# Attention products cut from 256 to 128 moving columns in a hybrid transformer layer

## The chip, the cores and the metric

The kernel runs on one core of a Trainium2 chip. The metric is the device time of one execution in microseconds (us). A lower time is better. All times of the profile come from one profiled execution, counted from its first instruction.

## The reference

One layer of a hybrid encoder on 512 tokens of width 1024, all in float32. What matters here is the token mixing: one input projection, three groups of attention heads of width 64, and one output projection.

```python
def reference(x, p, ln_mix, w_in, ...):
    hn = rms_norm(h, ln_mix[i])
    z = hn @ w_in[i]                      # columns of all head groups
    (q1, q2, k1, k2, va, qf, kf, vf, fg, qc, kc, vc) = jnp.split(z, IN_SPLITS, axis=-1)
    ...
    o_a = diff_attention(q1, q2, k1, k2, va, lam, subln_g, lam_init)   # 4 heads, two softmax maps each
    o_b = forgetting_attention(qf, kf, vf, log_f)                      # 6 heads, causal
    o_c = chunk_attention(qc, kc, vc, rel_bias[i])                     # 6 heads, chunk-causal
    h = h + jnp.concatenate([o_a, o_b, o_c], axis=-1) @ w_out[i]
    h = h + conv_gated_mlp(rms_norm(h, ln_ffn[i]), ...)                # width 2816, causal conv of width 3
    gate = jax.nn.sigmoid(rms_norm(h, ln_ple[i]) @ w_ple_gate[i])
    return h + (p[i] @ w_ple_proj[i]) * gate
```

Each attention is softmax(q k + bias) v with a mask that lets a token see its own block of 128 tokens (cut by the mask) and the blocks before it, and no later block.

## The kernel before, in words

**Stages.** The first stage multiplies the normalised input by the combined projection, runs the attention, and adds the output projection. The second is the gated MLP, and the last the gate with the per-layer embedding. The attention is spread over the projections of the first stage: while the projection of one pair of heads runs on TensorE, the attention of earlier pairs is mixed into the same stream. The pairs are A0, A1, B0, B1, B2, C0, C1 and C2, two heads each, so there are 16 heads.

**Precision.** Almost every product is made with operands of type float32r (`F32R`), each number split into a high part (names with `h`, `hi` or `th`) and a rest (`l`, `lo` or `tl`), and summed over two or three matmuls. In the profile `z<-whi,Th` is a matmul into the PSUM tile `z` with `whi` as the moving operand and `Th` as the stationary one. The profile shows the operands of F32R and of plain float32 alike as `f32`. Plain float32 is used by the transposes (moving operand `ident`) and by one small product, `o<-otmp,oall` in `subln` (line 966), which sums squares for the heads of group A and moves 512 columns.

**Scores** (`softmax_map`, lines 855 to 877). For a block `qb` of 128 queries, the keys up to `L = (qb + 1) * P` matter, with `P = 128`. Two matmuls write the scores to a bank `s`: one with the keys `k`, one with their rests `kl`. They move `N = max(L, 256)` key columns, so the first query block moves 256 columns, though only the first 128 are read afterwards. There are 8 such maps for each query block in group A (two maps for each of 4 heads), 6 in B and 6 in C: 20 in all, and so 40 matmuls for each of the four query blocks.

**Values** (`prob_cols` and `values`, lines 905 to 955). The probabilities are transposed to columns by key block. Key blocks 0 and 1 get tiles `pth` and `ptl` of their own (512 and 384 columns). Key blocks 2 and 3 share the tiles `ptc[0]` (high parts) and `ptc[1]` (rests): columns 0 to 127 hold zeros, written once at the start by two ScalarE activations (lines 834 and 835), columns 128 to 255 the one block of queries that sees key block 3, columns 256 to 511 the two that see key block 2. `values` sums the products of the four key blocks in one bank `o`, two matmuls for each key block. For key block 3 it moves columns 0 to 255 of `ptc`, zeros first, to columns 256 to 511 of `o` (`off = min(kb, 2) * P`). So each of the 16 heads has four matmuls from `ptc`, all 256 columns wide.

**What sets the order.** The class `Plan` records the operations of the first stage with their dependencies and then chooses an order for each engine, in `solve`. `price` (lines 194 to 227) gives each operation a duration; that of an F32R matmul is `n * 0.0004556 + 0.001` us for `n` moving columns, whatever `n` is. `due` gives every TensorE operation a due time from the sum of the durations ahead of it, plus a number for its group from the table `SHIFT`; the other engines' due times follow back from there. `emit` then issues all instructions in the order chosen, and each engine works through its own in that order. The later stages have a second plan, which takes over the clocks and memory of the first.

Of the kernel before, what the change touches and what calls it, by code (L numbers as in the profile page):

```python
# [11 lines left out]
AF = mybir.ActivationFunctionType  # L12
# [3 lines left out]
P = 128  # L16
# [309 lines left out]
def kernel(ctx: ExitStack, tc: tile.TileContext, x, xt0, xt, pt_in, small, g_ffn_in, bias_c,  # L326
# [8 lines left out]
    def f32(ap):  # L335
        return ap.bitcast(F32)
# [31 lines left out]
    pe, act, dve, pool, sp = (Engine(*e) for e in (("pe", nc.tensor), ("act", nc.scalar), ("dve", nc.vector), ("pool", nc.gpsimd), ("sp", nc.sync)))  # L368
# [45 lines left out]
    def bank(tag, name):  # L414
        return banks.tile([P, 512], F32, tag, {"z": 2, "s": 2, "t": 3, "o": 1}[tag])
# [14 lines left out]
    ident = cp.tile([P, P], F32, tag="ident", name="ident")  # L430
# [162 lines left out]
    for b in range(2):  # L593
        for i in range(2):
            c = HALF[1 - i]
# [11 lines left out]
    def done(*key):  # L607
        DONE.add(key)

    def need(*keys):  # L610
        for key in keys:
            assert key in DONE, key
# [218 lines left out]


    ptc = [ap.tile([P, S], F32R, tag=f"ptc{b}", name=f"ptc{b}") for b in range(2)]
    for b in range(2):
        act.activation(ptc[b][:, 0:P], ident, AF.Copy, scale=0.0)

    def head_bias(kind, hd):

# [15 lines left out]

    def softmax_map(m, hh, qb, bias, rowb, name):
        L = (qb + 1) * P
        N = max(L, 256)
        q, k, kl = m[0][hh], m[1][hh], m[2]
        c = slice(qb * P, L)
        sp = bank("s", f"{name}_s")  # L860
        pe.matmul(sp[:, :N], q[:, c], k[:, :N], start=True, stop=False)
        pe.matmul(sp[:, :N], q[:, c], kl[hh][:, :N], start=False, stop=True)
        e = ap.tile([P, L], F32, tag=f"e{qb}", bufs=2, name=f"{name}_e")
        st = ap.tile([P, 4], F32, tag="st", bufs=12, name=f"{name}_st")
        init = 3.0e38
        for n, (c0, tab) in enumerate(bias):
            c = slice(c0, c0 + tab.shape[1])
            acc = st[:, 3 * n : 3 * n + 1]
            dve.tensor_tensor_reduce(out=e[:, c], in0=sp[:, c], in1=tab, scale=-1.0, scalar=init,
                                           op0=ALU.add, op1=ALU.min, accum_out=acc)  # L870
            init = acc
        if rowb is not None:
            dve.scalar_tensor_tensor(st[:, 0:1], init, rowb, rowb, ALU.subtract, ALU.add)
            init = st[:, 0:1]
        act.activation(e, e, AF.Exp, scale=-1.0, bias=init, accum_out=st[:, 1:2])
        dve.reciprocal(st[:, 2:3], st[:, 1:2])
        return e, st
# [3 lines left out]
    def scores(pr, hh, qbs):  # L881
        kind, i = pr[0], int(pr[1])
        hd = 2 * i + hh
        if kind == "B":
            need(("fc",))
        if (pr, hh) not in BIAS:
            BIAS[pr, hh] = head_bias(kind, hd)
            PROB[pr, hh] = []
        for qb in qbs:
            bq = BIAS[pr, hh](qb)  # L890
            rowb = fq[:, qb, hd : hd + 1] if kind == "B" else None
            e, st = softmax_map(QK[pr, 0], hh, qb, bq, rowb, f"{pr}_{hh}_{qb}")
            if kind == "A":
                yield
                e2, st2 = softmax_map(QK[pr, 1], hh, qb, bq, rowb, f"{pr}_{hh}_{qb}b")
                pool.tensor_scalar(e2, e2, st2[:, 2:3], X["nlam"], ALU.mult, ALU.mult)
                dve.scalar_tensor_tensor(e, e, st[:, 2:3], e2, ALU.mult, ALU.add)
            else:
                pool.tensor_scalar(e, e, st[:, 2:3], 1.0, ALU.mult, ALU.mult)
            PROB[pr, hh].append(e)  # L900
            if hh == 1 and qb == NT - 1:
                KL_FREE.extend(QK[pr, part][2] for part in range(2) if (pr, part) in QK)
            yield

    def prob_cols(pr, hh):
        probs = PROB[pr, hh]
        tiles = []
        for kb in range(2):
            n = (NT - kb) * P
            pt = bank("t", f"{pr}_{hh}_pt{kb}")  # L910
            for qb in range(kb, NT):
                pe.transpose(pt[:, (qb - kb) * P : (qb - kb + 1) * P], probs[qb][:, kb * P : (kb + 1) * P], ident)
            th = ap.tile([P, S], F32R, tag="pth", bufs=3, name=f"{pr}_{hh}_pth{kb}")
            tl = ap.tile([P, S], F32R, tag="ptl", bufs=3, name=f"{pr}_{hh}_ptl{kb}")
            act.copy(th[:, :n], pt[:, :n])
            dve.tensor_tensor(out=tl[:, :n], in0=pt[:, :n], in1=f32(th[:, :n]), op=ALU.subtract)
            tiles.append((th[:, :n], tl[:, :n]))
            yield
        assert not PTC_OF
        PTC_OF.append((pr, hh))  # L920
        pt = bank("t", f"{pr}_{hh}_ptc")
        pe.transpose(pt[:, P : 2 * P], probs[3][:, 3 * P : 4 * P], ident)
        pe.transpose(pt[:, 2 * P : 3 * P], probs[2][:, 2 * P : 3 * P], ident)
        pe.transpose(pt[:, 3 * P : 4 * P], probs[3][:, 2 * P : 3 * P], ident)
        th, tl = ptc
        act.copy(th[:, P:], pt[:, P:])
        dve.tensor_tensor(out=tl[:, P:], in0=pt[:, P:], in1=f32(th[:, P:]), op=ALU.subtract)
        tiles.append((th[:, 2 * P :], tl[:, 2 * P :]))
        tiles.append((th[:, : 2 * P], tl[:, : 2 * P]))
        PT[pr, hh] = tiles  # L930
        yield

    def values(pr, hh):
        need(*(("in", pr, 0, t) for t in range(NT)))
        if pairs.index(pr) >= 6:
            need(("split", pairs.index(pr) - 6))
        if hh == 0:
            O[pr] = oall[:, pairs.index(pr) % 6, :]
        base = hh * HD
        po = bank("o", f"{pr}_{hh}_po")  # L940
        for kb in range(NT):
            off = min(kb, 2) * P
            v = V[pr][:, kb, hh * P : (hh + 1) * P]
            for j in range(2):
                pe.matmul(po[:, off:], v, PT[pr, hh][kb][j], start=kb == 0 and j == 0, stop=kb == 3 and j == 1)
            if kb % 2 == 1 and kb < 3:
                yield
        PTC_OF.remove((pr, hh))
        other = HD - base
        tmp = ap.tile([P, S], F32, tag="otmp", bufs=1, name=f"{pr}_{hh}_ot")  # L950
        act.copy(tmp[base : base + HD, :], po[other : other + HD, :])
        dve.tensor_tensor(out=O[pr][base : base + HD, :], in0=po[base : base + HD, :],
                                in1=tmp[base : base + HD, :], op=ALU.add)
        done("o" if kind_done(pr) else "o_raw", pr, hh)
        yield

    def kind_done(pr):
        return pr[0] != "A"
# [107 lines left out]
    for pr in ("A0", "A1"):  # L1066
        add(pr + "s01", scores, pr, 0, (0, 1))
        add(pr + "s02", scores, pr, 0, (2, 3))
        add(pr + "p0", prob_cols, pr, 0)
        add(pr + "v0", values, pr, 0)  # L1070
        add(pr + "s11", scores, pr, 1, (0, 1))
        add(pr + "s12", scores, pr, 1, (2, 3))
        add(pr + "p1", prob_cols, pr, 1)
        add(pr + "v1", values, pr, 1)
        add(pr + "n", subln, pr)
    for pr in ("B0", "B1", "B2", "C0", "C1", "C2"):
        add(pr + "v1", values, pr, 1)
    for pr in ("B0", "B1", "B2", "C0", "C1", "C2"):
        add(pr + "a", qk_cols, pr, 0)
        add(pr + "s0", scores, pr, 0, range(NT))  # L1080
        add(pr + "s1", scores, pr, 1, range(NT))
        add(pr + "p0", prob_cols, pr, 0)
        add(pr + "v0", values, pr, 0)
        add(pr + "p1", prob_cols, pr, 1)
# [17 lines left out]
    for j, (pr, part, *_) in enumerate(PARTS[1:], 1):  # L1102
        n = w_in[j].shape[3]
        for t in range(NT):
            run(f"in{j}_{t}", in_unit(pr, part, n, t, ws), steps.get(slot, []))
            slot += 1
            if slot >= 37:
                c = slice((slot - 37) * P, (slot - 36) * P)
# [3 lines left out]
        if j + 1 < len(PARTS):  # L1112
            q = PARTS[j + 1]
# [923 lines left out]
    while ready:  # L2037
        q = ready.pop()
# [26 lines left out]
    while order:  # L2065
# [3 lines left out]
        if now:  # L2069
            q = now[0]  # L2070
        else:
            tr = [(trial(q)[0], q) for q in can]
            first_at = max(min(x for x, _ in tr), clock["dve"])
            q = min((q for x, q in tr if x <= first_at + 0.1), key=lambda q: q.dl)

            late = min((q for x, q in tr if x <= first_at + SLACK), key=lambda q: q.dl)
            q = late if late.dl < q.dl - URGENT else q
# [70 lines left out]
```

## Time and profile before

| | us |
|---|---|
| median of 3 runs | 699.09 (698.72 to 699.47) |
| span of the profiled execution, first to last instruction | 697.6 |
| what lies outside the span (median less span) | about 1.5 |
| TensorE busy (PE) | 687.9 of 697.6 |
| VectorE busy (DVE) | 572.9 |
| ScalarE busy (ACT) | 423.5 |
| GpSimd busy (POOL) | 310.5 |

The profile gives the profiled execution's span and no separate time around it, so the median of the runs stands beside it. PE is TensorE's matmul stream and PEld its weight loads, which lie beside matmuls. The length of a single matmul record covers its way through the array, and neighbours overlap; what a matmul costs the stream is read from the distance between the starts of two records. Every instruction that goes through the recording layer has the line 360, so operations are told apart by their tiles.

### The profile page before, as it was taken

Reading aid. Unit: us, or ns where it says so; the run is one execution under the profiler, and the core shown is the slowest. Engines: PE = TensorE matmul, PEld = TensorE weight load, DVE = VectorE, ACT = ScalarE, POOL = GpSimd, SP = SyncE. Lnnn points to the kernel's source line nnn. Section 1 sums busy time; section 2 is a strip of 40 time slices with the busy share of each in tenths; the row PEclk is TensorE's granted clock in tenths of the full one; section 3 lists DMA queues with packets and bytes.
Section 4 is the critical chain, followed back from the end, with each engine's and each line's share of the span. In section 5 each row is a group of like instructions: output and inputs, shape, how many; then the busy total and the mean of one; then the engine's idle time right before and its main releaser. Section 6 shows DMA issues by size and latency. Waiting matters only on the chain.

```text
span 697.6 us, 12855 instructions
## 1 busy us (share of the span) xinstructions
PE 687.9 (99%) x4600; PEld 643.3 (92%) x4600; DVE 572.9 (82%) x1159; ACT 423.5 (61%) x812; POOL 310.5 (45%) x418
## 2 busy tenths in 40 slices
PE   7999999999999999999999999999999999999997
PEld 7999999999999888899988999898998898999997
DVE  6688899888887873888996988789898899777867
ACT  6657676666675672766755544556536676446853
POOL 3677676756764661222231333421622502344561
PEclk9999999999999999999999999999999999999999
DMA  9543354413222152585865338764368654132433
GB/s 310 204 128 92 87 149 129 110 64 92 88 62 72 61 114 98 192 240 127 218 162 145 110 93 224 162 187 129 93 176 224 169 159 128 48 105 67 150 117 122
DMA packets 42989, 94.31 MB, mean 135 GB/s; under 512 B 4871, under 2 KB 9607, under 8 KB 42925
## 3 DMA queue, kind: packets, MB, share of 16 engines
q1 hardware_dynamic: 35868, 79.02, 35.8%
q0 software_dynamic: 6768, 14.16, 11.6%
q8 instruction: 36, 0.59, 0.4%
q10 hardware_dynamic: 288, 0.30, 0.1%
q14 instruction: 29, 0.23, 0.1%
HBM read 85.20 MB, written 4.21 MB: 128 GB/s over the span
## 4 chain that ended last, share of the span: by engine, by line
PE 96%; DVE 1%; POOL 1%; DMA 0%; ACT 0%; issue 0%; POOLq 0%
PE z L360 45%; PE s L360 23%; PE t L360 20%; PE o L360 8%; DMA zn<-in_w_in_dram 0%; DVE xh_again L360 0%; POOL rs L360 0%; POOL e L360 0%; DVE xl_again L360 0%; DVE kl L360 0%; DVE rs L360 0%; ACT xh_again L360 0%; POOL wlo L360 0%; DVE oall L360 0%; ACT sq L360 0%
## 5 line engine op out<-in xcount | busy, mean ns | idle before, releaser
L360 ACT CAST whi<-wraw 128x768 fp32r<-128x768 f32 (+2 forms) x146 | 108.4, 761 | 49.2 <-DMA wraw<-in_w_up_dram 10.6
L360 DVE TENSOR_TENSOR wlo<-wraw,whi 128x768 fp32r<-128x768 f32 (+2 forms) x128 | 112.8, 893 | 18.1 <-ACT whi L360 16.2
L360 PE MATMUL z<-whi,Th 128*128 128x384 f32 (+2 forms) x360 | 120.3, 346 | 4.8 <-ACT whi L360 4.6
L360 PE MATMUL z<-wlo,Th 128*128 128x384 f32 (+2 forms) x360 | 119.6, 342 | 0.0
L360 PE MATMUL z<-whi,Tl 128*128 128x384 f32 (+2 forms) x360 | 119.3, 341 | 0.0
L360 PEld LDWEIGHTS z<-whi,Th 128*128 128x128 f32 x360 | 67.8, 190 | 8.4 <-ACT whi L360 4.9
L360 PEld LDWEIGHTS z<-whi,Tl 128*128 128x128 f32 x360 | 67.8, 189 | 2.9
L360 PEld LDWEIGHTS z<-wlo,Th 128*128 128x128 f32 x360 | 68.1, 190 | 2.3
L360 POOL TENSOR_TENSOR wraw<-wraw,wraw 128x768 f32<-128x768 f32 (+2 forms) x21 | 28.1, 1343 | 82.7 <-DVE pin L360 41.0
L360 ACT ACTIVATE e<-e,st 128x128 f32<-128x128 f32 (+3 forms) x80 | 44.6, 559 | 16.6 <-DVE st L360 16.3
L360 PE MATMUL z<-Th,whi 128*128 128x256 f32 (+1 forms) x152 | 51.8, 341 | 0.0
L360 PE MATMUL z<-Tl,whi 128*128 128x256 f32 (+1 forms) x152 | 51.6, 340 | 0.0
L360 PE MATMUL z<-Th,wlo 128*128 128x256 f32 (+1 forms) x152 | 51.5, 340 | 0.0
L360 PE MATMUL s<-Tl,whi 128*128 128x256 f32 (+1 forms) x152 | 51.5, 340 | 0.0
L360 PE MATMUL s<-Th,wlo 128*128 128x256 f32 (+1 forms) x152 | 51.3, 340 | 0.0
L360 PE MATMUL s<-Th,whi 128*128 128x256 f32 (+1 forms) x152 | 51.1, 341 | 0.0
L360 POOL TENSOR_TENSOR rs<-rs,nhalf 128x4 f32<-128x4 f32 x40 | 43.2, 1090 | 4.9 <-DVE rs L360 1.4
L360 DVE CUSTOM_DVE_ANT_0 e<-s,bias 128x128 f32<-128x128 f32 (+3 forms) x74 | 33.9, 471 | 5.4 <-PE s L360 2.8
L360 POOL TENSOR_SCALAR e<-e,st 128x256 f32<-128x256 f32 (+3 forms) x48 | 29.1, 641 | 10.3 <-DVE st L360 8.3
L360 POOL DMA_DIRECT2D wraw<-in_w_up_dram x21 | 18.9, 902 | 31.4 <-DMA wraw<-in_w_up_dram 21.4
L360 PE MATMUL t<-whi,al 128*128 128x256 f32 x116 | 32.2, 282 | 0.0
L360 PE MATMUL t<-wlo,ah 128*128 128x256 f32 x116 | 32.1, 281 | 0.0
(342 smaller groups left out, 2286.6 us busy)
## 6 DMA issues: line engine op xcount, KB each, us to landing
wraw<-in_w_up_dram SPq DMA_DIRECT2D x41, 384.0 KB, 4.5
wraw<-in_w_in_dram SPq DMA_DIRECT2D x28, 384.0 KB, 3.6
wraw<-in_w_down_dram SPq DMA_DIRECT2D x17, 384.0 KB, 3.2
wlo_again<-in_w_up_dram SPq DMA_DIRECT2D x12, 384.0 KB, 4.3
whi_again<-in_w_up_dram SPq DMA_DIRECT2D x11, 384.0 KB, 4.5
wraw<-in_w_out_dram SPq DMA_DIRECT2D x16, 256.0 KB, 2.8
wraw<-in_w_up_dram SPq DMA_DIRECT2D x16, 256.0 KB, 3.9
wlo<-wraw POOLq DMA_DIRECT2D x7, 384.0 KB, 4.8
```

What stands on the lines that cost most here:

```text
L360: ins = getattr(self.eng, op)(*a, **k)
```

## The change

Three things change. The scores of the first query block move 128 key columns instead of 256. The value product of key block 3 moves its own 128 columns to columns 384 to 511 of the bank, instead of 256 columns that begin with zeros. And the two activations that wrote the zeros are gone. That concerns 2 matmuls in each of 20 first-block maps and 2 in each of 16 heads: 72 matmuls. The number of matmuls stays.

```diff
     ptc = [ap.tile([P, S], F32R, tag=f"ptc{b}", name=f"ptc{b}") for b in range(2)]
-    for b in range(2):
-        act.activation(ptc[b][:, 0:P], ident, AF.Copy, scale=0.0)
...
     def softmax_map(m, hh, qb, bias, rowb, name):
         L = (qb + 1) * P
-        N = max(L, 256)
...
-        pe.matmul(sp[:, :N], q[:, c], k[:, :N], start=True, stop=False)
-        pe.matmul(sp[:, :N], q[:, c], kl[hh][:, :N], start=False, stop=True)
+        pe.matmul(sp[:, :L], q[:, c], k[:, :L], start=True, stop=False)
+        pe.matmul(sp[:, :L], q[:, c], kl[hh][:, :L], start=False, stop=True)
...
-        tiles.append((th[:, : 2 * P], tl[:, : 2 * P]))
+        tiles.append((th[:, P : 2 * P], tl[:, P : 2 * P]))
...
         for kb in range(NT):
-            off = min(kb, 2) * P
+            off = kb * P
```

Since `price` goes by the number of columns, the plan of the first stage comes out in another order as well. On TensorE the order of the tile names differs from the first scores of A0 to the last heads, some 1600 rows into the program; the rows behind that, the MLP and the gate, are the same. VectorE, ScalarE and GpSimd move rows too, and SyncE exchanges a few loads with their neighbours.

TensorE, the first scores of head 0 of pair A0, mixed with the projection of A1. `s_131` is the score bank, `k_154` and `kl_0_100` the keys and their rests, `q_151` the queries, `z_129` the projection's bank:

```order
 L360 MATMUL z_129<-whi_110,Th_64 128x384
-L360 MATMUL s_131<-k_154,q_151 128x256
+L360 MATMUL s_131<-k_154,q_151 128x128
 L360 MATMUL z_129<-wlo_111,Th_64 128x384
-L360 MATMUL s_131<-kl_0_100,q_151 128x256
+L360 MATMUL s_131<-kl_0_100,q_151 128x128
 L360 MATMUL z_129<-whi_110,Tl_66 128x384
 L360 MATMUL z_129<-whi_112,Th_65 128x384
 L360 MATMUL z_129<-wlo_113,Th_65 128x384
 L360 MATMUL z_129<-whi_112,Tl_67 128x384
+L360 MATMUL z_129<-whi_112,Th_65 128x384
 L360 MATMUL s_131<-k_154,q_151 128x256
```

The first two rows of scores stand where they stood, at half the width; the scores of the second query block follow one projection matmul later.

TensorE, the last transposes of the probabilities of head 0 of A0 (tiles `t`, from the probabilities `e`) and the head's first value product (`o_148<-pth_172`), before:

```order
L360 MATMUL t_149<-ident,e_0_95 128x128 x2
L360 MATMUL z_128<-wlo_124,Th_65 128x256
L360 MATMUL z_128<-whi_123,Tl_67 128x256
L360 MATMUL z_128<-whi_126,Th_65 128x256
L360 MATMUL z_128<-wlo_127,Th_65 128x256
L360 MATMUL z_128<-whi_126,Tl_67 128x256
L360 MATMUL o_148<-pth_172,V_142 128x512
```

The same place in the changed kernel:

```order
L360 MATMUL t_149<-ident,e_0_93 128x128
L360 MATMUL t_149<-ident,e_0_95 128x128
L360 MATMUL o_148<-pth_172,V_142 128x512
L360 MATMUL o_148<-ptl_173,V_142 128x512
L360 MATMUL o_148<-pth_174,V_142 128x384
L360 MATMUL o_148<-ptl_175,V_142 128x384
L360 MATMUL o_148<-ptc_0_137,V_142 128x256
L360 MATMUL z_128<-whi_117,Th_64 128x256
L360 MATMUL z_128<-wlo_118,Th_64 128x256
```

The projection matmuls that stood between the transposes and the value products now stand behind the value products. `pth` is ScalarE's copy of the transposed probabilities and `ptl` VectorE's difference; both are made between the transpose and the product that moves them.

## Prediction

> **What bounds the kernel now.** I read the page first, then the waits of TensorE, then the table by stage. From the page, the span, the busy times and the shares of the chain that ended last:
>
> ```profile
> span 697.6 us, 12855 instructions
> PE 687.9 (99%) x4600; PEld 643.3 (92%) x4600; DVE 572.9 (82%) x1159; ACT 423.5 (61%) x812; POOL 310.5 (45%) x418
> ...
> PE 96%; DVE 1%; POOL 1%; DMA 0%; ACT 0%; issue 0%; POOLq 0%
> ```
>
> The waits of TensorE, as engine and tile waited for, then us in total, times, and the longest:
>
> ```profile
> PE z L360 <- ACT whi L360: 4.6, 1, 4.6
> PE t L360 <- DVE zn L360: 0.2, 1, 0.2
> ```
>
> The windows are the start, the stage in which attention and projections are mixed, and the rest. Columns: us, then busy us of PE, PEld, DVE, ACT and POOL, each with its count, the granted clock, DMA share and GB/s.
>
> ```profile
> 0.00:41.00 41.00, 36.38 (x226) 36.26 (x227) 29.68 (x69) 27.54 (x54) 20.64 (x40) 1.00 0.71 247
> 41.00:280.00 239.00, 238.58 (x1433) 220.92 (x1432) 191.18 (x561) 152.86 (x374) 152.90 (x237) 1.00 0.34 93
> 280.00:697.60 417.60, 412.95 (x2944) 386.14 (x2943) 352.06 (x530) 243.13 (x386) 136.98 (x142) 1.00 0.54 148
> ```
>
> The reader is to see that TensorE sets the time, and in the very stage that the change touches: 238.58 of 239.00 us, at the full clock, with VectorE next at 191.18. Its one long wait is at the start, for the first weights. So each nanosecond that a matmul of this stage gains or loses is, to first order, a nanosecond of the total. The question is what a 128-column F32R product costs the stream, and what the new order adds.
>
> **The products: 72 of them.** Those of the present kernel, by shape (count, then busy us and mean ns of one):
>
> ```profile
> L360 PE MATMUL o<-ptc,V 128*128 128x256 f32 x64 | 17.0, 296 | 0.0
> L360 PE MATMUL s<-k,q 128*128 128x256 f32 x40 | 11.4, 309 | 0.1
> L360 PE MATMUL s<-kl,q 128*128 128x256 f32 x40 | 10.8, 298 | 0.0
> ```
>
> Half of each group changes: the 32 products of key block 3 out of 64, and the first query block's 20 and 20 out of 40 and 40. The second half of the score groups is the second query block, 256 wide by itself. In the new order the 72 rows stand as 128x128, so the change does what it says.
>
> What one costs today is the distance between starts, in the timeline (start, length, instruction):
>
> ```profile
> 65.01 0.28 PE L360 MATMUL o<-ptc,V 128*128 128x256 f32 x1
> 65.13 0.28 PE L360 MATMUL z<-whi,Th 128*128 128x256 f32 x1
> 65.25 0.28 PE L360 MATMUL o<-ptc,V 128*128 128x256 f32 x1
> 65.36 0.28 PE L360 MATMUL z<-wlo,Th 128*128 128x256 f32 x1
> ```
>
> Three of them take 65.36 - 65.01 = 0.35 us: 117 ns each. The trace holds no F32R product narrower than 256 columns, so the new cost has to be bounded from rows beside it. A 512-wide F32R pair, and the one plain float32 product of 512 columns (two records, then the next instruction):
>
> ```profile
> 56.06 0.40 PE L360 MATMUL s<-k,q 128*128 128x512 f32 x1
> 56.30 0.40 PE L360 MATMUL s<-kl,q 128*128 128x512 f32 x1
> 56.53 0.27 PE L360 MATMUL t<-ident,e 128*128 128x128 f32 x1
> ...
> 153.84 1.02 PE L360 MATMUL o<-otmp,oall 128*128 128x512 f32 x2
> 154.70 0.60 PE L360 MATMUL t<-ident,e 128*128 128x128 f32 x4
> ```
>
> The only records that move 128 columns are transposes, here three of them among 256-wide projection products:
>
> ```profile
> 72.97 0.28 PE L360 MATMUL z<-wlo,Th 128*128 128x256 f32 x1
> 73.09 0.28 PE L360 MATMUL t<-ident,e 128*128 128x128 f32 x1
> 73.12 0.36 PE L360 MATMUL z<-whi,Tl 128*128 128x256 f32 x1
> 73.33 0.27 PE L360 MATMUL t<-ident,e 128*128 128x128 f32 x1
> 73.35 0.36 PE L360 MATMUL z<-whi,Th 128*128 128x256 f32 x1
> 73.56 0.27 PE L360 MATMUL t<-ident,e 128*128 128x128 f32 x1
> 73.58 0.37 PE L360 MATMUL z<-wlo,Th 128*128 128x256 f32 x1
> 73.78 0.28 PE L360 MATMUL z<-whi,Tl 128*128 128x256 f32 x1
> ```
>
> And the weight load that goes ahead of each of these products (minimum, median and maximum ns):
>
> ```profile
> L360 PEld LDWEIGHTS o<-ptc,V x64: 186/188/193, 63.7 to 276.8; 128*128 128x128 f32 x64
> ```
>
> That gives four prices for a 128-wide product, worked out one by one:
> - *It streams at its width.* 512 columns cost 56.53 - 56.06 = 0.47 us for two, 235 ns each; 256 cost 117 ns. That is 0.46 ns a column, so 128 cost 59 ns. Each saves 58 ns: 72 x 58 = 4.2 us less.
> - *It costs what the other 128-wide records cost.* From 72.97 to 73.78 there are four products of 117 ns and three transposes: (0.81 - 0.47) / 3 = 113 ns. 72 x 4 = 0.3 us less.
> - *The weight load shows.* If the shortened product no longer hid any of its load of 188 ns, each would cost 71 ns more: 5.1 us more.
> - *It costs what a float32 product costs.* 154.70 - 153.84 = 0.86 us for 512 columns is 1.68 ns a column, 215 ns for 128. Each costs 98 ns more: 72 x 98 = 7.1 us more.
>
> I take the last. The trace shows two rates for products of four-byte operands, 0.46 and 1.68 ns a column. The fast one belongs to the F32R form, and only from 256 columns up; even the 128-wide transposes, which only move data, take 113 ns, 0.88 ns a column, as much as nearly twice as many F32R columns. Nothing shows the fast rate holding at 128, so I read it as bound to wide operands, with the f32 product as the row nearest in kind below. This is a choice, not a reading, and the other three prices stay as ends.
>
> The Trainium skill, "TensorE: Matmul & The Clock Gate", section "Back-to-back issue gap", speaks against this choice: it gives a sustained spacing of about 81 ns for 128 columns and 131 ns for 512, with no word on the operand type. By it the 72 products would cost 72 x (117 - 81) = 2.6 us less, an estimate. The trace disagrees at 512 columns, where the spacing is 235 ns. The same page, section "LDWEIGHTS (loading the stationary operand)", puts a load of 128 columns at 128 / 1.2 = 107 ns whatever follows; taken as a floor, that would be an estimated saving of 0.7 us, and no run here shows such a floor.
>
> **The zeros.** The two removed activations lie at the start of ScalarE, ahead of the weights' first cast:
>
> ```profile
> 2.95 0.51 ACT L360 ACTIVATE ptc<-ident 128x128 fp32r<-128x128 f32 x2
> 4.06 0.51 ACT L360 CAST whi<-zn 128x384 fp32r<-128x384 f32 x1 [0.60 <-DMA zn<-in_w_in_dram]
> ```
>
> They end at 3.46, and the cast then idles 0.60 us for its DMA. They cost nothing now and gain nothing when they go.
>
> **The new order.** The plan prices a 128-wide product at half, so all due times behind the first one move, and with them TensorE's rows to the end of the attention; the loads that SyncE exchanges are weights and head biases of the same stage. In the present order, head 0 of A0 looks like this from its last transposes to its value products:
>
> ```profile
> 61.72 0.49 PE L360 MATMUL t<-ident,e 128*128 128x128 f32 x3
> 61.96 0.36 PE L360 MATMUL z<-wlo,Th 128*128 128x256 f32 x1
> ...
> 62.63 0.40 PE L360 MATMUL o<-pth,V 128*128 128x512 f32 x1
> ...
> 63.22 0.44 PE L360 MATMUL o<-ptl,V 128*128 128x512 f32 x1
> ```
>
> From the end of the last three transposes (61.96) to the product that needs both ScalarE's copy and VectorE's difference there are 1.3 us, filled with projection products. The new order puts some four transposes (4 x 113 ns) and one 512-wide product (235 ns) there, 0.7 us of work. So TensorE would wait about 0.6 to 0.7 us at this place, with everything queued behind it, projection products included. Heads whose first value product stands directly behind a transpose of probabilities number five in the new order and one in the old. Four such waits would be 2.8 us; but waits elsewhere can go, and the stage's whole visible idle is 239.00 - 238.58 = 0.4 us. I take 0.7 us, with ends -0.4 and +2.8. Slower products fill part of such waits, which is why I don't take more. A wait of the other engines that changes costs nothing here as long as TensorE has rows to run.
>
> **The sum.** Against the profiled execution: 697.6 + 7.1 + 0.7 = 705.4 us of span. The median of the runs is 699.09, 1.5 us above that span, so the forecast is 699.1 + 7.8 = **706.9 us**. Its own range goes from 5.1 - 0.4 (the weight load's price, no new wait) to 7.1 + 2.8: 703.8 to 709.0.
>
> **The rivals.**
> - *It streams at its width (faster).* The place is the same 72 products, at 59 ns: 699.1 - 4.2 + 0.7 = 695.6 us. For it speaks that 256 and 512 columns cost the same per column, with no fixed part to be seen. Against it, the 128-wide transposes are off that line by 54 ns. It decides for faster once a product costs under 117 - 700 / 72 = 107 ns, and beyond what can be measured under 88 ns. The Trainium skill's 81 ns in the section named above would lie here. Chance 0.15.
> - *The price of the other 128-wide records (no change).* 113 ns: 699.1 - 0.3 + 0.7 = 699.5 us. For it speaks that the record is equally wide and has a 128 x 128 load of its own; against it, that a transpose is not the same operation. Chance 0.12.
> - *The order decides (slower, at a small price of the products).* At 113 ns with four waits of 0.7 us: 699.1 - 0.3 + 2.8 = 701.6 us. Chance 0.03, since the changed stretch of the program is otherwise full of projection products that can fill.
>
> **How the numbers follow.** My forecast has a chance of 0.70. A difference of 0.2%, 1.4 us, is about what a measurement of this kernel can tell from no change. Slower by more: 0.70 + 0.03 = 0.73; within it: 0.12; faster by more: 0.15. The range reaches from the no-change case with its idle gone (699.1 - 0.3 - 0.4 = 698.4) to the upper end of the forecast's own, 709.0; it leaves out the faster rival and some 0.05 at the ends.
>
> **What would show it.** Right: in the timeline, the start after a 128-wide `s<-k,q` or `o<-ptc,V` comes some 0.21 us later; TensorE's busy time in the attention stage grows by about 7 us at the same number of matmuls; the last stage keeps its length. Around the first value product of A0 a gap of about 0.7 us appears. Wrong: a distance near 0.06 us (streaming) or 0.11 us (the transposes' price); or a distance as I expect and new waits of TensorE of several us beside it; or the last stage, whose TensorE rows are unchanged, changing its length.

## The result and the profile after

The changed kernel takes 710.62 us (median of 4 runs, 709.79 to 711.70) against 699.28 us before (4 runs, 698.72 to 699.61). The ratio is 1.0163, with a 95% interval of 1.0148 to 1.0177: slower by 11.3 us. The forecast was 706.9 us, and its range ended at 709.0.

From the page of the changed kernel, the same lines as before:

```profile
span 708.6 us, 12849 instructions
PE 691.9 (98%) x4600; PEld 643.0 (91%) x4600; DVE 572.3 (81%) x1159; ACT 423.3 (60%) x810; POOL 311.7 (44%) x418
...
PE 91%; DVE 3%; DMA 2%; ACT 1%; POOL 1%; issue 1%; POOLq 0%; ACTq 0%
```

The span grew by 11.0 us, TensorE's busy time only by 4.0, and in the chain that ended last other engines now hold a share. So TensorE waits. The longest of its waits, as engine and tile waited for, us in total, times, longest:

```profile
PE z L360 <- ACT whi L360: 4.5, 1, 4.5
PE s L360 <- DVE st L360: 1.9, 5, 0.8
PE s L360 <- POOL k L360: 1.0, 1, 1.0
PE z L360 <- DVE zn L360: 0.8, 1, 0.8
PE t L360 <- DVE e L360: 0.7, 1, 0.7
PE o L360 <- DVE ptl L360: 0.7, 3, 0.3
PE t L360 <- DVE ptc L360: 0.6, 1, 0.6
PE t L360 <- DVE zn L360: 0.6, 1, 0.6
```

The first is the wait for the first weights, which was there before. The others are new, but for 0.2 us of the last: many short waits, for softmax results (`st`, `e`), for keys, for normalised projections (`zn`) and for parts of the probabilities. The table by stage places them (us, then busy us of PE, PEld, DVE, ACT and POOL):

```profile
41.00:280.00 239.00, 231.55 (x1383) 211.49 (x1382) 185.46 (x554) 149.28 (x368) 151.11 (x226) 1.00 0.33 89
```

In the same 239 us TensorE ran 1383 matmuls instead of 1433 and stood idle for 7.4 us instead of 0.4. The busy time hides some of the loss, since a record's tail covers the start of a wait: the three transposes at 59.28 further down are 3 x 0.113 = 0.34 us of work, and their record lasts 0.49 us. How much the whole stage lost is read from the start of the last value product; the rows give minimum, median and maximum ns, and the first and last start. Before:

```profile
L360 PE MATMUL o<-ptc,V x64: 277/281/367, 63.9 to 276.9; 128*128 128x256 f32 x64
```

After:

```profile
L360 PE MATMUL o<-ptc,V x64: 218/279/368, 63.0 to 287.7; 128*128 128x256 f32 x32, 128*128 128x128 f32 x32
```

The last one starts 10.8 us later. From there to the end the kernel takes 697.6 - 276.9 = 420.7 us before and 708.6 - 287.7 = 420.9 us after. All but 0.2 us of the loss lies in the attention stage. The granted clock has next to no part in it: its mean over the span is 0.998 against 0.999, some 0.7 us of 709.

What a narrow product costs stands in the timeline of the changed kernel, at two value products among projection products:

```profile
64.28 0.22 PE L360 MATMUL o<-ptc,V 128*128 128x128 f32 x1
64.34 0.33 PE L360 MATMUL z<-wlo,Th 128*128 128x256 f32 x1
64.51 0.23 PE L360 MATMUL o<-ptc,V 128*128 128x128 f32 x1
64.57 0.33 PE L360 MATMUL z<-whi,Tl 128*128 128x256 f32 x1
```

The record after a narrow product starts early and runs longer, so the pair has to be read: from one narrow product to the next are 0.23 us, for one narrow and one 256-wide product. The wide one takes 0.117, which leaves 0.11 us for the narrow one. It is neither dearer nor markedly cheaper than at 256 columns.

The place that the prediction spoke of, head 0 of A0 from its last transposes to its value products, in the same timeline:

```profile
59.28 0.49 PE L360 MATMUL t<-ident,bias 128*128 128x128 f32 x3
60.48 0.77 PE L360 MATMUL t<-ident,e 128*128 128x128 f32 x5 [0.71 <-DVE e L360]
61.56 0.49 PE L360 MATMUL o<-pth,V 128*128 128x512 f32 x1 [0.32 <-ACT pth L360]
62.29 0.50 PE L360 MATMUL o<-ptl,V 128*128 128x512 f32 x1 [0.23 <-DVE ptl L360]
62.62 0.34 PE L360 MATMUL o<-pth,V 128*128 128x384 f32 x1
62.80 0.40 PE L360 MATMUL o<-ptl,V 128*128 128x384 f32 x1
63.03 0.28 PE L360 MATMUL o<-ptc,V 128*128 128x256 f32 x1
63.22 0.39 PE L360 MATMUL z<-whi,Th 128*128 128x256 f32 x1
```

From 59.28 to 63.22 are 3.94 us. The matmuls in it are worth 8 x 0.113 + 2 x 0.235 + 2 x 0.18 (62.62 to 62.80) + 0.117 = 1.85 us. TensorE lost 2.1 us here, for three reasons in a row: the last probabilities, then ScalarE's copy, then VectorE's difference. The last two, 0.32 + 0.23 = 0.55 us of visible idle, are the wait that the prediction put at 0.6 to 0.7 us; the first it did not count. VectorE's rows tell why the probabilities were late:

```profile
58.06 0.33 DVE L360 SCALAR_TENSOR_TENSOR e<-e,st,e 128x128 f32<-128x128 f32 x1
59.35 0.42 DVE L360 TENSOR_REDUCE rs<-sq 128x4 f32<-128x256 f32 x1 [0.96 <-ACT sq L360]
59.68 0.74 DVE L360 SCALAR_TENSOR_TENSOR e<-e,st,e 128x512 f32<-128x512 f32 x1
```

The 512-wide `e` for which TensorE waited is queued behind a reduction that waits 0.96 us for ScalarE's squares. With the order fixed ahead, such a row holds what stands behind it, on this engine and then on TensorE.

### The profile page after: what moved, and what is told of

Same layout as the page of the kernel before. It is cut to its first block, busy times and chain, and to the rows that moved or that the text cites. A ratio compares the mean times of both kernels' runs of the same rounds, so it can differ in the third digit from the quotient of the medians.

```text
span 708.6 us, 12849 instructions
## 1 busy us (share of the span) xinstructions
PE 691.9 (98%) x4600; PEld 643.0 (91%) x4600; DVE 572.3 (81%) x1159; ACT 423.3 (60%) x810; POOL 311.7 (44%) x418
## 4 chain that ended last, share of the span: by engine, by line
PE 91%; DVE 3%; DMA 2%; ACT 1%; POOL 1%; issue 1%; POOLq 0%; ACTq 0%
PE z L360 43%; PE s L360 22%; PE t L360 18%; PE o L360 8%; DMA wraw<-in_w_up_dram 1%; DVE e L360 1%; DMA zn<-in_w_in_dram 0%; POOL k L360 0%; DVE xh_again L360 0%; ACT whi L360 0%; DVE ptl L360 0%; ACT sq L360 0%; POOL whi_again L360 0%; DVE xl_again L360 0%; DVE rs L360 0%
## 5 line engine op out<-in xcount | busy, mean ns | idle before, releaser
L360 ACT ACTIVATE e<-e,st 128x384 f32<-128x384 f32 (+3 forms) x80 | 44.7, 560 | 24.4 <-DVE st L360 24.1
L360 POOL TENSOR_TENSOR rs<-rs,nhalf 128x4 f32<-128x4 f32 x40 | 45.1, 1157 | 5.4 <-DVE rs L360 2.0
L360 POOL TENSOR_SCALAR e<-e,st 128x256 f32<-128x256 f32 (+3 forms) x48 | 27.4, 593 | 15.7 <-DVE st L360 14.2
```

Of the source, the lines that this page charges most:

```text
L360: ins = getattr(self.eng, op)(*a, **k)
```

## The experiments

After the first reading two theories stood. The **order theory**: a narrow product costs about what the wide one did, and the 11 us come from the order that the plan made anew. The **product theory**, that of the prediction: the narrow products cost the time themselves or through what waits for them. Each comparison is with runs of the kernel before on the same chip.

**Narrow products in the old order.**

```diff
-                op.busy = n * 0.0004556 + 0.001 if op.ins[0].dtype == F32R else n * 0.0017
+                op.busy = max(n, 256) * 0.0004556 + 0.001 if op.ins[0].dtype == F32R else n * 0.0017
```

> The changed kernel, with 128-wide products and no zeros, but the plan prices an F32R matmul of under 256 columns like one of 256, so every engine keeps the order of the kernel before. Order theory (a 128-wide product costs the stream about 114 ns, as the distances in the changed kernel's timeline say, and the 11 us come from waits that the new order brings): 72 x (114 - 117) ns = -0.2 us, so 0.2 us under the kernel before, and the waits of TensorE in the attention stage as before. Product theory (the narrow products bring the time, by themselves or by what waits for them, as the prediction had it): 7 to 11 us over the kernel before.

Measured: 698.0 us against 698.93, ratio 0.9989 (0.9981 to 0.9998). In its trace all rows of TensorE, VectorE and GpSimd stand in the order of the kernel before, and TensorE's waits are the same:

```profile
PE z L360 <- ACT whi L360: 4.6, 1, 4.6
PE t L360 <- DVE zn L360: 0.2, 1, 0.2
```

All that the change does to the work is in this kernel, and it gains 0.8 us (by the ratio; 0.9 by the medians), less than the 0.2% that the prediction called measurable. The product theory falls.

**Wide products in the new order.** The plan is told 128 columns for the 72 products, which move 256 as before.

```diff
+NARROW = [0]
...
+                n = NARROW[0] or n
                 op.busy = n * 0.0004556 + 0.001 if op.ins[0].dtype == F32R else n * 0.0017
...
+        NARROW[0] = L
         pe.matmul(sp[:, :N], q[:, c], k[:, :N], start=True, stop=False)
         pe.matmul(sp[:, :N], q[:, c], kl[hh][:, :N], start=False, stop=True)
+        NARROW[0] = 0
...
+                NARROW[0] = P if kb == 3 else 0
                 pe.matmul(po[:, off:], v, PT[pr, hh][kb][j], start=kb == 0 and j == 0, stop=kb == 3 and j == 1)
+                NARROW[0] = 0
```

> The kernel before, with 256-wide products and the zeros, but the plan prices the 72 products as if they had 128 columns, so every engine gets the order of the changed kernel. Order theory: as slow as the changed kernel, 10 to 12 us over the kernel before, with the same waits of TensorE. Product theory: 0 to 4 us over the kernel before, the part that the order had in the prediction.

Measured: 711.82 us against 698.93, ratio 1.0184 (1.0170 to 1.0198), 12.9 us more. The rows of TensorE, VectorE and GpSimd stand in the order of the changed kernel, and the waits repeat almost to the number; these follow the wait for the first weights (two added lines move the line numbers by two):

```profile
PE s L362 <- DVE st L362: 2.2, 6, 0.8
PE s L362 <- POOL k L362: 1.0, 1, 1.0
PE z L362 <- DVE zn L362: 0.8, 1, 0.8
PE o L362 <- DVE ptl L362: 0.7, 3, 0.3
PE t L362 <- DVE e L362: 0.6, 1, 0.6
```

So the order alone, with not one product changed, makes the whole loss. With the run before, this is shown from both sides. The loss is 1.6 us above that of the changed kernel; 0.8 of it fits what the narrow width gained in the old order, the rest is open.

**The products at 64 columns, in the old order.** The edit is against the kernel before. The two activations that write the zeros stay in this kernel, though nothing reads the zeros.

```diff
-                op.busy = n * 0.0004556 + 0.001 if op.ins[0].dtype == F32R else n * 0.0017
+                op.busy = max(n, 256) * 0.0004556 + 0.001 if op.ins[0].dtype == F32R else n * 0.0017
...
-        N = max(L, 256)
+        W = L if qb else HD
...
-        pe.matmul(sp[:, :N], q[:, c], k[:, :N], start=True, stop=False)
-        pe.matmul(sp[:, :N], q[:, c], kl[hh][:, :N], start=False, stop=True)
+        pe.matmul(sp[:, :W], q[:, c], k[:, :W], start=True, stop=False)
+        pe.matmul(sp[:, :W], q[:, c], kl[hh][:, :W], start=False, stop=True)
...
-        tiles.append((th[:, : 2 * P], tl[:, : 2 * P]))
+        tiles.append((th[:, P + HD : 2 * P], tl[:, P + HD : 2 * P]))
...
-            off = min(kb, 2) * P
+            off = kb * P if kb < 3 else S - HD
```

> The order of the kernel before, with the 72 products at 64 columns: half of the first block's keys, and half of the queries that see key block 3, are left out, so its time tells of the products' width alone. If a product costs at least the time of its weight load (the order theory's reading of 114 ns): within 0.4 us of the kernel with 128 columns in the same order. If a product streams at its width, with the load hidden: 72 x 29 ns = 2.1 us less than with 128 columns. If it cost a float32 product's 1.68 ns a column: 7.7 us less.

Measured: 698.57 us, ratio 0.9993 (0.9984 to 1.0002), against 698.0 us with 128 columns on the same chip: 0.3 us more by the ratios, 0.6 by the medians, and the two intervals overlap. The timeline has the same two products:

```profile
64.06 0.20 PE L360 MATMUL o<-ptc,V 128*128 128x64 f32 x1
64.09 0.36 PE L360 MATMUL z<-whi,Th 128*128 128x256 f32 x1
64.29 0.19 PE L360 MATMUL o<-ptc,V 128*128 128x64 f32 x1
64.31 0.36 PE L360 MATMUL z<-wlo,Th 128*128 128x256 f32 x1
```

Again 0.23 us from one narrow product to the next. Half the columns save nothing: there is a floor of about 0.11 us for such a product. That the floor is the weight load fits PEld: beside a narrow product of the changed kernel the loads start 0.11 us apart (52.02 and 52.13), and in its whole trace only some 2 loads in 100 start less than 0.108 us behind the one before. But no run varied the load itself, so that part is argued.

**The plan with the true price.** Was the new order bad because the plan took the products for half of what they cost?

```diff
-                op.busy = n * 0.0004556 + 0.001 if op.ins[0].dtype == F32R else n * 0.0017
+                op.busy = max(n * 0.0004556 + 0.001, 0.1145) if op.ins[0].dtype == F32R else n * 0.0017
```

> The changed kernel, with the plan's price of an F32R matmul not under 0.1145 us, the cost read from the changed kernel's timeline, instead of 0.0593. The plan comes out in a third order. Wrong-price theory (the new order is bad because the plan took the 72 products for half of what they cost, 4 us in all): 699 to 700.5 us, waits nearly gone. Table theory (the due times of the table fit one order, and any plan that comes out otherwise loses that fit): 3 to 11 us over the kernel before, though the price is right.

Measured: 707.26 us against 698.93, ratio 1.0125 (1.0109 to 1.0142), 8.3 us more. The price is right now, and it differs from that of 256 columns by a mere 3 ns a product; the plan still comes out in another order, and that order waits too. The wrong-price theory falls. What is left is that the plan's order and the table `SHIFT` belong together; the runs without the table, below, try that.

**No product changed at all, another price.**

```diff
-                op.busy = 0.109
+                op.busy = 0.1145
```

> The kernel before, with all its 256-wide products and its zeros; only the plan's price of a transpose goes from 0.109 to 0.1145 us, which is nearer to the 0.113 us of the trace. No matmul changes, but the plan comes out in another order. Table theory (the table of shifts fits one order, and any change of the plan's times loses that fit): 3 to 11 us over the kernel before. Rival (only an order made with too low a price for the 72 products is bad, or the 7 us of the kernel with the true price have to do with its narrow products): within 1.5 us of the kernel before.

Measured: 715.47 us against 698.94, ratio 1.0236 (1.0221 to 1.0252), 16.5 us more, beyond the 11 expected. A better price for the transposes, with the work untouched, costs more than the change did. It reaches beyond the first stage too, since the later plan also holds transposes: the last value product starts at 291.3, 14.4 us later than before, in a span that is 17.0 us longer.

**Without the table.** The plan of the first stage is the one with `late` at zero. It gets only the shifts from `rest` on, none of which is for its groups.

```diff
-        self.due(SHIFT)
+        keys = list(SHIFT)
+        self.due(SHIFT if self.late else {k: SHIFT[k] for k in keys[keys.index("rest"):]})
```

> The kernel before, with the table's shifts for the first stage left out (all zero) and nothing else changed. It tells what the table is worth: table theory, 5 to 20 us over the kernel before, at least as much as the change cost, since all of the fit is gone. If the table's shifts are worth little, so that losing their fit can't explain 11 us: under 3 us over the kernel before.

Measured: 705.72 us against 698.94, ratio 1.0097 (1.0080 to 1.0114), 6.8 us more. So the shifts are worth 6.8 us in the plan that they go with. The expectation that losing all of the fit would cost at least as much as the change was wrong: the changed kernel, whose table no longer fits, loses more than a kernel without one.

**The changed kernel without the table.** The same edit on the changed kernel.

> The changed kernel, with the table's shifts for the first stage left out. The kernel before without them stands 6.8 us over the kernel before. Table theory (the shifts help only in the plan they were made for, and do harm in another): 4 to 10 us over the kernel before, so under the changed kernel with its table (11.3 us over). Rival (the low price itself makes the plan bad, whatever the table): as far over the kernel without a table as the changed kernel is over the kernel before, 15 to 20 us over the kernel before.

Measured: 705.25 us against 699.38, ratio 1.0082 (1.0067 to 1.0097), 5.9 us more. Narrow or wide, and with either price, a plan without the table stands 6 to 7 us over the kernel before, and the two intervals overlap. TensorE's last 2864 rows are the same in all three kernels; they begin 5.4 us later than before with wide products and 5.2 with narrow ones, so the attention stage loses the same in both. The low price does no harm by itself; with the table it does 11.3.

**Due times and the plan's clock apart.** `op.wide` is the price at 256 columns. First the due times as before:

```diff
+                op.wide = max(n, 256) * 0.0004556 + 0.001 if op.ins[0].dtype == F32R else n * 0.0017
...
-                t += op.busy
+                t += getattr(op, "wide", op.busy)
```

> The changed kernel, with the 72 products priced at 256 columns in the sum that makes the due times, and at 128 columns in the plan's clock, which decides what is ready when. If the loss comes from due times that moved against the table's shifts: within 2 us of the kernel before. If it comes from the plan's clock, which then takes tiles as ready later or earlier than they are on the chip: 7 to 13 us over the kernel before. If either alone loses the fit: 3 to 11 us, here and in the kernel with the reverse.

Then the plan's clock as before:

```diff
-            busy = op.busy * (1.85 if e == "pe" and t0 < 8.6 else 1.0)
+            busy = getattr(op, "wide", op.busy) * (1.85 if e == "pe" and t0 < 8.6 else 1.0)
```

> The reverse of the one just told: the changed kernel, with the 72 products priced at 128 columns in the sum that makes the due times, and at 256 in the plan's clock. If the due times carry the loss: 7 to 13 us over the kernel before. If the clock does: within 2 us. If either alone loses the fit: 3 to 11 us in both.

Measured: 718.39 us against 698.94, ratio 1.0274 (1.0257 to 1.0292), 19.4 us more, and 704.39 us, ratio 1.0079 (1.0064 to 1.0094), 5.4 us more. Neither half brings the time of before back, so the table fits only with both together. The first loss lies well over what any theory here gave. A part of it is the clock, below: its mean of 0.990 over a span of 717.7 us can account for some 7 us at most.

**Each part alone.** The scores alone (`N = L` instead of `N = max(L, 256)`), then the value products and the zeros alone:

> Only the scores of the first query block move 128 columns, 40 products; the value products and the zeros stay as before, and the plan prices by columns, so it makes an order of its own. Table theory: a loss of 3 to 17 us, of no set relation to the number of products. Rival (the loss comes with the number of products priced too low): 40 of 72 of the changed kernel's loss, 5.5 to 7 us.

> Only the value product of key block 3 moves 128 columns, 32 products, and the zeros are gone; the scores stay as before, and the plan prices by columns. Table theory: a loss of 3 to 17 us, of no set relation to the number of products, and the two parts' losses needn't add up to that of the whole. Rival (by the number of products priced too low): 32 of 72 of the changed kernel's loss, 4.5 to 6 us.

Measured: 714.68 us against 699.38, ratio 1.0226 (1.0197 to 1.0255), 15.3 us more; and 710.02 us, ratio 1.0150 (1.0133 to 1.0167), 10.6 us more. Each half costs about as much as the whole or more, and they don't add up to it (25.9 against 11.3). A loss by the number of products would have been 5.5 to 7 and 4.5 to 6 us. The clock has a part here too: in the four runs of the scores alone its mean lay between 0.996 and 0.987, and the run with 0.987 is the slowest, 718.3 us.

Seven plans, that of the changed kernel among them, had the table and another price. Six lost more (8.3 to 19.4 us) than the two without the table (5.9 and 6.8), and the one with the plan's clock as before lost 5.4. So a table that no longer fits does more harm than none in most of these plans, not in all. The loss does not follow the size of the change of price either: 72 x 3 ns gave 8.3 us, 72 x 58 ns gave 11.3.

## Why the prediction was wrong

- *TensorE bounds the stage that changes.* Right. The whole loss is there, and the rest of the program kept its length to 0.2 us.
- *The price of a product, 215 ns.* Wrong, and it is the first step that failed: "I read it as bound to wide operands, with the f32 product as the row nearest in kind below". Measured is 0.11 us, against 0.117 at 256 columns. The row nearest in width was the right one, the 128-wide transposes with 113 ns. The float32 price also took two records for one: the 0.86 us are two records (`x2`), 0.84 ns a column each, while a narrow F32R product stays one record (4600 matmuls before and after). The term of 7.1 us was in truth some -0.3 us (0.23 - 0.117 = 0.113 us, 72 x 4 ns), and the old-order run shows -0.8 (-1.3 to -0.1).
- *The Trainium skill's two prices.* "TensorE: Matmul & The Clock Gate", section "Back-to-back issue gap", gave 81 ns; the trace has 0.11 us, so it did not hold for these products. The 107 ns of "LDWEIGHTS (loading the stationary operand)", taken as a floor, came near: the record of a load lasts 0.19 us here, but loads start as little as 0.11 us apart, and the run at 64 columns shows that there is a floor.
- *The order, 0.7 us, at most 2.8.* This is the second step that failed, by its size: the order by itself costs 12.9 us. The mechanism was seen and its place was right, but that one place lost 2.1 us, not 0.7, because VectorE's own rows were late as well. Waits of kinds that I didn't count (for `st`, `zn`, `k`) make up some 4 of the 6 us of visible idle elsewhere. I counted one pattern, value products directly behind transposes, and took everything else as filled; of the five heads with this pattern only this one shows more than 0.02 us of idle time before its first value product (0.32 us). The rival "the order decides" had the right cause; it had a chance of 0.03, and its 701.6 us are 9 us short.
- *Why the chance was so small.* "The changed stretch of the program is otherwise full of projection products that can fill." They can fill only where the order puts them. The order before left 0.4 us of visible idle because its table of shifts went with its plan; I read that as a property of the stage.
- *The zeros cost nothing.* Nothing contradicts it: the kernel with the old order leaves them out and gains 0.8 us in all. They weren't tried alone.
- *Direction.* Slower was right, but by luck: the 7.1 us that were to make it so did not come, and an order term of 0.7 alone, with the products at their measured price, would have been no change.

## What to carry to other kernels

Where a planner with a tuned table sets the order, a change of size is two changes: that of the work, and that of every order that follows from its price. Time them apart, by giving the planner the old price; here that turned a loss of 11.3 us into a gain of 0.8 (0.1 to 1.3), and the kernel so made is the fastest complete one of the study. And a stage with no idle time can lose that with its order: ask what made it so, and whether the change keeps it.

## What the runs showed of the hardware

Narrow F32R products have a floor: 64 and 128 columns cost the same, about 0.11 us, and 256 cost 0.117. At 0.46 ns a column the floor is what some 240 columns cost, an estimate, so in this kernel cutting such a product below that would save nothing.

A cluster of waits can cost twice. In the run with the due times as before, at 185 us (5 us each; PE busy first, the granted clock third from the end):

```profile
180.00:185.00 5.00, 5.00 (x31) 5.00 (x30) 0.35 (x1) 0.37 (x1) 0.00 (x0) 1.00 0.00 0
185.00:190.00 5.00, 2.73 (x13) 1.57 (x12) 3.62 (x7) 3.14 (x7) 3.29 (x6) 0.88 0.00 0
190.00:195.00 5.00, 5.00 (x18) 4.81 (x19) 3.70 (x16) 0.58 (x1) 2.90 (x4) 0.50 0.00 0
195.00:200.00 5.00, 5.00 (x34) 4.97 (x33) 2.70 (x15) 4.15 (x12) 2.28 (x5) 0.94 0.23 52
```

After a stretch with TensorE busy for 2.73 of 5 us, the granted clock is 0.50 for the next five. Projection products of 384 columns then start 0.32 us apart (193.41 and 193.73), where they started 0.17 us apart before (184.06 and 184.23). The Trainium skill, "TensorE: Matmul & The Clock Gate", section "What's actually happening", has the clock fall to half after an idle window of about 3.4 us; this trace agrees on the half, with 0.50, but the pauses of TensorE here were 1.45, 0.57 and 0.24 us, with matmuls between them.

Such a stretch does not always bring the clock down. In the kernel with the plan's clock as before, one wait of 2.04 us falls into the first of these windows, and the clock stays at 1.00:

```profile
150.00:155.00 5.00, 2.96 (x14) 2.00 (x13) 4.40 (x19) 3.03 (x8) 1.28 (x2) 1.00 0.31 103
155.00:160.00 5.00, 5.00 (x33) 4.90 (x33) 3.23 (x15) 4.62 (x16) 2.85 (x5) 1.00 0.00 0
```

What decides between the two is not shown. In the changed kernel itself the mean clock stayed at 0.998.
